# Weight sums of a seven-product layer in another order, and the down products' operands made in pieces between products

## The chip, the cores and the metric

One core of one Trainium2 chip runs one launch of the kernel. The metric is the device time of that launch in microseconds (us), the median over the runs shown. Engines are named as in the profile: PE (matrix unit), PEld (its weight loads), DVE (vector), ACT (scalar), POOL (GpSimd), SP (the queue that issues most DMAs).

## What is computed

The reference is one layer of a decoder for 1024 prompt tokens and 8 x 4 decode tokens, 1056 in all, model width 1024, everything in float32. Cut to the part in which the change lies:

```
mix = concat([attention(...), pooling(...)]) @ w_out
x = x + rms(mix, n_mix_post)
f = rms(x, n_ffn_pre)
f = (silu(f @ w_gate) * (f @ w_up)) @ w_down        # 1024 -> 2816 -> 1024
x = x + rms(f, n_ffn_post)
x = x + sigmoid(x @ w_ple_gate) * (p @ w_ple)
```

## The kernel before, in words

Tokens lie in three groups of 352 columns (g = 0, 1, 2). Features lie on the 128 partitions. Every float32 factor is split into a rounded part and a rest (`split`, line 172: a cast on ACT, then a difference on DVE), and a product term is three matmuls: part by part, part by rest, rest by part. One matmul is 128x128 by 128x352.

For groups 0 and 1 the products run two by two in a fast scheme with seven products in place of eight (`seven`, line 1085). The left matrix A has four blocks: the row is one 128-column chunk of `w_gate` (first raw tile, `a1`) or of `w_up` (second raw tile, `a2`), the column is one half of the 1024 inputs. The right matrix B has the input half as its row and the token group as its column. The seven products of such a **pair** are taken in this order: A11 B11, A12 B21, A22 T4, S2 T2, S3 T3, S1 T1, S4 B22, with S1 = A21+A22, S2 = S1-A11, S3 = A11-A21, S4 = A12-S2 (`T1` to `T4` are sums of the right side, made once). Each product is 12 matmuls (`product`), so a pair is 84. Group 2 uses plain products (`do_one`, `do_dn_one`).

The 22 chunks of the hidden width are worked in slabs of four (`SLAB`). In a slab s of the pair stage, the steps are pair 0, pair 1, down pair 0, pair 2, down pair 1, pair 3: 6 x 84 = 504 matmuls. A **down pair** (`do_dn_pair`, line 1199) multiplies the hidden values of slab s-1 by `w_down`, again with seven products, each in two halves of six matmuls, and adds each half to an accumulator in SBUF (`ap`; by DVE at line 1221, in the first slab by ACT at line 1223). Two pairs of a last, short slab and the last two down pairs end the stage. The names in the profile: `wr` is a raw weight tile, `wh`/`wl` the split of the whole first tile, `w` the split of A22 (the half product), `sh`/`sl` the split of the sums, `fh`/`fl` the right side, `hf` the hidden values of groups 0 and 1, `hp` the operands made of them for the down pairs, `b` a PSUM bank (8 of them).

**Weights.** SP loads raw tiles of 512 KB into three buffers in turn; the split tiles lie in eight buffers in turn. `need` makes the items four ahead of the one that is used: the sums of a pair are made during the pair before. `w_sums` (line 1044) runs four POOL operations in place (line 1054), two sums into each raw tile, then splits the two tiles (lines 1056 to 1059).

**Order.** PE's products are kept in program order. On the other engines a scheduler of the framework places the instructions when the kernel is built; each engine then runs its own list strictly in order. A wait of one instruction holds all behind it.

**Operands of the down pairs.** After pair 3 of a slab `h_operands` (line 1134) makes seven operands, B11, B21, B22 and the sums T1, T3, T2, T4: seven ACT casts, seven DVE differences (`hp`) and four DVE sums into `hf` (line 1131).

**Chains.** Work that should run between products can be written as a generator. `chain` registers it; `turn(n)`, called after every product, moves a counter on by n and lets a generator whose time has come issue its next piece; its next due time is its load divided by `share[0]`. `finish` issues at once what is left.

The functions that the change touches, and what calls them, are printed here with the line numbers of the profile:

Of the kernel before, what the change touches and what calls it, by code (L numbers as in the profile page):

```python
# [13 lines left out]
ALU = mybir.AluOpType  # L14
# [23 lines left out]
NSLAB = FFC // SLAB  # L38
# [24 lines left out]
def trunk_kernel(  # L63
# [33 lines left out]
    te, ve, se, ge = nc.tensor, nc.vector, nc.scalar, nc.gpsimd  # L97
# [14 lines left out]
    def act_tile(shape, dt=F32, s="a"):  # L112
        return apool.tile(shape, dt, tag="a", bufs=A_SLOTS, name=nm(s))

    def half(g, dt=F32, s="h"):
        return act_tile([P, 4, NS[g]], dt, s)
# [15 lines left out]
    def bank():  # L132
        return psum.tile([P, 512], F32, tag="b", name=nm("b"))
# [38 lines left out]
    def split(hi, lo, src):  # L172
        fix(se.copy(hi, src))  # L173
        fix(ve.tensor_tensor(lo, src, hi.bitcast(F32), op=ALU.subtract))  # L174
# [11 lines left out]
    def w_tile(shape, s):  # L186
        return wpool.tile(shape, F32R, tag="wp", bufs=2 * W_PAIRS, name=nm(s))
# [127 lines left out]
    def need(k, ahead=LOOK):  # L315

        for i in range(len(made), min(k + ahead + 1, len(ITEMS))):
            kind, js = ITEMS[i]
            if kind == "direct":
                w_split(js[0])  # L320
                made[i] = pairs[js[0]]
            elif kind == "half":
                w_load(js[0])
                hl = two_in_one([P, 4, P])
                split(*hl, raws[js[0]][:, 4:8, :])
                made[i] = hl
            elif kind == "small":
                w_load(js[0])
                hl = two_in_one([P, 2, 256])
                split(*hl, raws[js[0]])  # L330
                made[i] = hl
            else:
                made[i] = w_sums(*(raws[ITEMS[j][1][0]] for j in js))
            for kind, js in ITEMS[i + 1 : i + 3]:
                if kind != "sums":
                    w_load(js[0])
        return made[k]

    def gemm(ps, ops, start=True, stop=True):

        last = len(ops) - 1
        for i, (wh, wl, xh, xl) in enumerate(ops):
            mm(ps, wh, xh, start=start and i == 0, stop=False)
            mm(ps, wh, xl, start=False, stop=False)
            mm(ps, wl, xh, start=False, stop=stop and i == last)
# [589 lines left out]
    chains = []  # L935

    share = [0.6]

    def turn(n):

        now[0] += n
        for ch in [ch for ch in chains if ch[2]] or list(chains):
            while ch in chains and ch[1] <= now[0]:
                try:
                    load, wait = next(ch[0])
                except StopIteration:
                    chains.remove(ch)
                    break
                dve[0] = max(dve[0], now[0]) + load / share[0]
                ch[1] = dve[0] + wait  # L950

    def chain(steps, wait=0, alone=False):

        chains.append([steps, now[0] + wait, alone])

    def finish(ch_list):
        for ch in ch_list:
            for _ in ch[0]:
                pass
            chains.remove(ch)  # L960
# [83 lines left out]
    def w_sums(a1, a2):  # L1044


        a11, a12, a21, a22 = a1[:, 0:4, :], a1[:, 4:8, :], a2[:, 0:4, :], a2[:, 4:8, :]
        for out, a, b, op in (
            (a22, a21, a22, ALU.add),
            (a21, a11, a21, ALU.subtract),  # L1050
            (a11, a22, a11, ALU.subtract),
            (a12, a12, a11, ALU.subtract),
        ):
            ge.tensor_tensor(out, a, b, op=op)  # L1054
        two = []
        for src in (a1, a2):
            hl = w_tile([P, KC, P], "sh"), w_tile([P, KC, P], "sl")
            split(*hl, src)
            two.append(hl)
        (s24, s31) = two  # L1060
        return {"S2": quarter(s24, 0), "S4": quarter(s24, 1), "S3": quarter(s31, 0), "S1": quarter(s31, 1)}

    def ops4(w, x):

# [2 lines left out]
    def quarter(w, h):  # L1067
        return tuple(t[:, 4 * h : 4 * h + 4, :] for t in w)
# [16 lines left out]
    def seven(items, x7, done):  # L1085

        ig, iu, is_ = items[:3]
        wg = need(ig)
        p1 = tmp(N, "p1")
        se.copy(p1, product(quarter(wg, 0), x7["B11"]))  # L1090
        c11 = tmp(N, "c11")
        add(c11, p1, product(quarter(wg, 1), x7["B21"]))
        done("C11", c11)
        p4 = product(need(iu), x7["T4"])
        s = need(is_)
        add(p1, p1, product(s["S2"], x7["T2"]))
        u3 = tmp(N, "u3")
        add(u3, p1, product(s["S3"], x7["T3"]))
        c21 = tmp(N, "c21")
        add(c21, u3, p4)  # L1100
        done("C21", c21)
        p5 = product(s["S1"], x7["T1"])
        add(u3, u3, p5)
        add(p1, p1, p5)
        done("C22", u3)
        add(p1, p1, product(s["S4"], x7["B22"]))
        done("C12", p1)
# [7 lines left out]
    def hid_put(g, s, i, ht):  # L1115
        if (g, s) not in hid:
            if s < NSLAB:
                hid[g, s] = half(g, F32R, "hid"), half(g, F32R, "hid")
            else:
                t = half(g, F32R, "hid")  # L1120
                hid[g, s] = t[:, :REST, :], t[:, REST : 2 * REST, :]
        hi, lo = hid[g, s]
        split(hi[:, i, :], lo[:, i, :], ht)

    def h_operand(name, src):
        t = act_tile([P, 2, 2, N], F32R, "hp")
        split(t[:, 0], t[:, 1], src)
        h7[name] = t[:, 0], t[:, 1]

    def h_sum(name, out, a, b):  # L1130
        ve.tensor_tensor(out, a, b, op=ALU.subtract)
        h_operand(name, out)

    def h_operands():
        b11, b21, b12, b22 = (hidf[g][:, 2 * k : 2 * k + 2, :] for g in (0, 1) for k in range(2))
        h_operand("B11", b11)
        h_operand("B21", b21)
        h_operand("B22", b22)
        h_sum("T1", b11, b12, b11)
        h_sum("T3", b12, b22, b12)  # L1140
        h_sum("T2", b22, b22, b11)
        h_sum("T4", b21, b21, b22)

    def do_pair(s, i, items):

        t = {}

        def done(which, c):
            t[which] = c
            if which in ("C11", "C12"):  # L1150
                se.activation(c, c, AF.Silu)
            if which == "C11" and i == 0 and s < NSLAB:
                for g in (0, 1):
                    hidf[g] = half(g, s="hf")
            for g, a, b in ((0, "C21", "C11"), (1, "C22", "C12")):
                if which == ("C21", "C12")[g]:
                    if s < NSLAB:
                        ve.tensor_tensor(hidf[g][:, i, :], t[a], t[b], op=ALU.mult)
                    else:
                        ve.tensor_tensor(t[a], t[a], t[b], op=ALU.mult)  # L1160
                        hid_put(g, s, i, t[a])

        seven(items, f7, done)
        if s < NSLAB and i == SLAB - 1:
            h_operands()

    def do_one(s, i, items):
        if (s, i) == (AHEAD, 0):
# [28 lines left out]
    accp = {}  # L1197

    def do_dn_pair(s, j, items):
        ia, ib, is_ = items  # L1200
        for at, which, h, x in (
            (1, ia, 0, "B11"),
            (2, ia, 1, "B21"),
            (4, ib, None, "T4"),
            (6, is_, "S2", "T2"),
            (7, is_, "S3", "T3"),
            (5, is_, "S1", "T1"),
            (3, is_, "S4", "B22"),
        ):
            w = need(which)  # L1210
            w = w if h is None else w[h] if which == is_ else quarter(w, h)
            xh, xl = h7[x]
            if at not in accp:
                accp[at] = half(0, s="ap")
            for r in range(2):
                ps = bank()
                gemm(ps[:, :N], [(w[0][:, 2 * c + r, :], w[1][:, 2 * c + r, :], xh[:, c, :], xl[:, c, :]) for c in range(2)])
                turn(6)
                o = accp[at][:, 2 * j + r, :]
                if s:  # L1220
                    ve.tensor_tensor(o, o, ps[:, :N], op=ALU.add)  # L1221
                else:
                    se.copy(o, ps[:, :N])  # L1223
# [10 lines left out]

    def do_spill():
        finish(list(chains))

    def do_spill_sums():
        for d, t in zip(osd, os_[2]):
            nc.sync.dma_start(d, t)  # L1240
# [113 lines left out]
    def do_ple_one(m, wp, w):  # L1354
# [6 lines left out]
    do = {  # L1361
        "one": do_one,
        "pair": do_pair,
        "dn_one": do_dn_one,
        "dn_pair": do_dn_pair,
        "dn_rest": do_dn_rest,
        "combine": do_combine,
# [99 lines left out]
```

## Time and profile before

| what | value |
|---|---|
| three runs, median (lowest to highest) | 1133.71 us (1133.09 to 1134.46) |
| the profiled execution, its own time | 1133.11 us |
| its span, first to last instruction | 1131.3 us |
| busy: PE, PEld, DVE, ACT, POOL | 1097.9, 1074.9, 843.6, 505.5, 262.4 us |
| mean granted TensorE clock | 0.989 |

A busy PE is not a PE at its peak: a matmul is shown with 0.32 us, though the next one starts 0.16 us after it. So idle time shows only where a gap is long, and time lost is better read from how many matmuls a stretch holds. "Idle before, releaser" is the time in which an engine stood still before an instruction, and what ended it.

### The profile page before, as it was taken

The page shows a single profiled execution, that of the slowest core. Times are in us where ns is not written, and L with a number is a line of the kernel's source. Part 1 is how long each engine was busy: PE and PEld are TensorE (multiplying, and loading weights), DVE is VectorE, ACT ScalarE, POOL GpSimd, SP SyncE. Part 2 cuts the span into 40 slices and gives each one's busy share as a digit, 9 for nine tenths or more (in the row PEclk, how much of TensorE's full clock was granted, in tenths as well). Part 3 has the DMA queues.
Part 4 walks back from the last instruction along what each step waited for, and adds up shares of the span by engine and source line. Part 5 has one row for each costly group of instructions (what it writes and reads, how often), then busy time and mean ns, then how long its engine had stood idle before and what let it go on. Part 6 is the DMA issues. An engine that isn't in the chain of part 4 may idle for free. (4 is left out here: it accounts for less than half of the span.)

```text
span 1131.3 us, 17864 instructions
## 1 busy us (share of the span) xinstructions
PE 1097.9 (97%) x6979; PEld 1074.9 (95%) x6979; DVE 843.6 (75%) x1298; ACT 505.5 (45%) x863; POOL 262.4 (23%) x212
## 2 busy tenths in 40 slices
PE   9999999999999999989989989989988999999998
PEld 9999988899999999989989989989987999999998
DVE  6776578877969766765677777777788987968973
ACT  7322377655555433435433433333344364444441
POOL 0072132100000123243343343343332000012300
PEclk9999999999999999999999989999999999999999
DMA  8121311634633324222212212212234456553362
GB/s 285 59 71 52 106 57 39 204 132 145 233 131 131 112 97 142 75 75 76 75 66 84 76 40 92 76 54 75 76 100 164 153 182 214 190 202 105 132 190 75
DMA packets 43573, 131.29 MB, mean 116 GB/s; under 512 B 5060, under 2 KB 15588, under 8 KB 43488
## 3 DMA queue, kind: packets, MB, share of 16 engines
q1 hardware_dynamic: 42160, 128.38, 33.4%
q10 hardware_dynamic: 1328, 1.77, 0.5%
q8 instruction: 55, 0.90, 0.3%
q14 instruction: 30, 0.25, 0.1%
HBM read 114.25 MB, written 15.87 MB: 115 GB/s over the span
## 5 line engine op out<-in xcount | busy, mean ns | idle before, releaser
L1054 POOL TENSOR_TENSOR wr<-wr 128x512 f32<-128x512 f32 x72 | 101.9, 1415 | 650.3 <-DVE w L174 647.5
L173 ACT CAST wh<-wr 128x1024 fp32r<-128x1024 f32 (+1 forms) x138 | 142.0, 1030 | 153.7 <-PE b L128 75.1
L128 PE MATMUL b<-fh,wh 128*128 128x352 f32 x624 | 201.6, 323 | 1.4 <-ACT ap L1223 1.4
L128 PE MATMUL b<-fh,wl 128*128 128x352 f32 x624 | 200.2, 321 | 0.0
L128 PE MATMUL b<-fl,wh 128*128 128x352 f32 x624 | 200.0, 320 | 0.0
L174 DVE TENSOR_TENSOR wl<-wr,wh 128x1024 fp32r<-128x1024 f32 (+1 forms) x138 | 168.0, 1218 | 33.7 <-ACT wh L173 32.6
L174 DVE TENSOR_TENSOR sl<-wr,sh 128x1024 fp32r<-128x1024 f32 x72 | 87.4, 1222 | 125.5 <-ACT sh L173 121.7
L173 ACT CAST sh<-wr 128x1024 fp32r<-128x1024 f32 x72 | 72.9, 1048 | 193.7 <-POOL wr L1054 193.7
L128 PE MATMUL b<-fh,sh 128*128 128x352 f32 x416 | 138.8, 334 | 13.1 <-ACT sh L173 12.2
L128 PE MATMUL b<-fh,sl 128*128 128x352 f32 x416 | 138.1, 332 | 3.7 <-DVE sl L174 3.7
L128 PE MATMUL b<-fl,sh 128*128 128x352 f32 x416 | 137.1, 329 | 0.0
L128 PEld LDWEIGHTS b<-fh,wh 128*128 128x128 f32 x624 | 117.0, 188 | 1.7 <-ACT ap L1223 1.7
L128 PEld LDWEIGHTS b<-fl,wh 128*128 128x128 f32 x624 | 117.4, 188 | 0.0
L128 PEld LDWEIGHTS b<-fh,wl 128*128 128x128 f32 x624 | 117.0, 188 | 0.0
L128 PE MATMUL b<-h,wh 128*128 128x352 f32 x480 | 105.7, 327 | 0.3 <-ACT h L426 0.3
L1054 POOL TENSOR_TENSOR wr<-wr,wr 128x512 f32<-128x512 f32 x72 | 102.2, 1420 | 5.6
L128 PE MATMUL b<-hid,wh 128*128 128x352 f32 x416 | 99.5, 322 | 0.0
L128 PEld LDWEIGHTS b<-fh,sh 128*128 128x128 f32 x416 | 81.1, 195 | 15.1 <-ACT sh L173 14.0
L128 PEld LDWEIGHTS b<-fh,sl 128*128 128x128 f32 x416 | 81.1, 195 | 5.6 <-DVE sl L174 5.6
L128 PE MATMUL b<-hp,sh 128*128 128x352 f32 x320 | 78.9, 329 | 7.5 <-DVE ap L1221 4.2
L128 PEld LDWEIGHTS b<-h,wh 128*128 128x128 f32 x480 | 82.7, 191 | 1.1 <-ACT h L426 0.6
L128 PEld LDWEIGHTS b<-fl,sh 128*128 128x128 f32 x416 | 81.4, 196 | 0.0
(195 smaller groups left out, 2231.5 us busy)
## 6 DMA issues: line engine op xcount, KB each, us to landing
wr<-in_w_gu_dram SPq DMA_DIRECT2D x88, 512.0 KB, 3.4
wr<-in_w_dn_dram SPq DMA_DIRECT2D x40, 512.0 KB, 3.3
wr<-in_w_pg_dram SPq DMA_DIRECT2D x16, 512.0 KB, 3.6
x<-in_x_dram SPq DMA_DIRECT2D x6, 704.0 KB, 9.3
x1d<-x SPq DMA_DIRECT2D x6, 704.0 KB, 3.5
x<-x1d SPq DMA_DIRECT2D x6, 704.0 KB, 5.5
out_y_dram<-yo SPq DMA_DIRECT2D x24, 176.0 KB, 2.9
wr<-in_w_out_b_dram SPq DMA_DIRECT2D x8, 512.0 KB, 3.8
```

The lines of the kernel that those rows point to most:

```text
L128: ins = te.matmul(*args, **kw)
L173: fix(se.copy(hi, src))
L174: fix(ve.tensor_tensor(lo, src, hi.bitcast(F32), op=ALU.subtract))
L1054: ge.tensor_tensor(out, a, b, op=op)
```

## The change

In `w_sums` the four sums are written in another way and order: S3 = A11-A21 and then S2 = A22-S3, both into the second raw tile, which is split at once; then S1 = A11+S2 and S4 = A12-S2 into the first raw tile, split second. S2 and S3, which PE takes first, lie in one split tile, S1 and S4 in the other. The order of PE's products is the same. `h_operands` becomes a generator of seven pieces, registered as a chain after pair 3 and finished at the latest at C21 (the fifth product) of the next slab's pair 0, where now also the new `hf` tiles are taken, or ahead of down pair 0. From the spill on, `share[0]` is 0.9.

```diff
         a11, a12, a21, a22 = a1[:, 0:4, :], a1[:, 4:8, :], a2[:, 0:4, :], a2[:, 4:8, :]
-        for out, a, b, op in (
-            (a22, a21, a22, ALU.add),
-            (a21, a11, a21, ALU.subtract),
-            (a11, a22, a11, ALU.subtract),
-            (a12, a12, a11, ALU.subtract),
+        two = []
+        for src, steps in (
+            (a2, ((a21, a11, a21, ALU.subtract), (a22, a22, a21, ALU.subtract))),
+            (a1, ((a11, a11, a22, ALU.add), (a12, a12, a22, ALU.subtract))),
         ):
-            ge.tensor_tensor(out, a, b, op=op)
-        two = []
-        for src in (a1, a2):
+            for out, a, b, op in steps:
+                ge.tensor_tensor(out, a, b, op=op)
             hl = w_tile([P, KC, P], "sh"), w_tile([P, KC, P], "sl")
             split(*hl, src)
             two.append(hl)
-        (s24, s31) = two
-        return {"S2": quarter(s24, 0), "S4": quarter(s24, 1), "S3": quarter(s31, 0), "S1": quarter(s31, 1)}
+        s32, s14 = two
+        return {"S2": quarter(s32, 1), "S4": quarter(s14, 1), "S3": quarter(s32, 0), "S1": quarter(s14, 0)}
...
     def h_operands():
         b11, b21, b12, b22 = (hidf[g][:, 2 * k : 2 * k + 2, :] for g in (0, 1) for k in range(2))
-        h_operand("B11", b11)
-        h_operand("B21", b21)
-        h_operand("B22", b22)
-        h_sum("T1", b11, b12, b11)
-        h_sum("T3", b12, b22, b12)
-        h_sum("T2", b22, b22, b11)
-        h_sum("T4", b21, b21, b22)
+        for name, b in (("B11", b11), ("B21", b21), ("B22", b22)):
+            h_operand(name, b)
+            yield 6, 0
+        for name, *args in (
+            ("T1", b11, b12, b11),
+            ("T3", b12, b22, b12),
+            ("T2", b22, b22, b11),
+            ("T4", b21, b21, b22),
+        ):
+            h_sum(name, *args)
+            yield 11, 0
...
-            if which == "C11" and i == 0 and s < NSLAB:
-                for g in (0, 1):
+            if which == "C21" and i == 0:
+                finish(list(chains))
+                for g in (0, 1) if s < NSLAB else ():
                     hidf[g] = half(g, s="hf")
...
         if s < NSLAB and i == SLAB - 1:
-            h_operands()
+            chain(h_operands(), 6)
...
     def do_dn_pair(s, j, items):
+        if j == 0:
+            finish(list(chains))
...
     def do_spill():
         finish(list(chains))
+        share[0] = 0.9
```

**On POOL**, these are the sums of two pairs, pair 0 and pair 1 of slab 4 (`wr_7100` and `wr_7235` hold `w_gate`, `wr_7146` and `wr_7280` hold `w_up`). Before:

```order
L1054 TENSOR_TENSOR wr_7146<-wr_7146 128x512
L1054 TENSOR_TENSOR wr_7146<-wr_7100,wr_7146 128x512
L1054 TENSOR_TENSOR wr_7100<-wr_7146,wr_7100 128x512
L1054 TENSOR_TENSOR wr_7100<-wr_7100 128x512
L1054 TENSOR_TENSOR wr_7280<-wr_7280 128x512
L1054 TENSOR_TENSOR wr_7280<-wr_7235,wr_7280 128x512
L1054 TENSOR_TENSOR wr_7235<-wr_7280,wr_7235 128x512
L1054 TENSOR_TENSOR wr_7235<-wr_7235 128x512
```

The same two groups in the changed kernel:

```order
L1054 TENSOR_TENSOR wr_7146<-wr_7100,wr_7146 128x512
L1054 TENSOR_TENSOR wr_7146<-wr_7146 128x512
L1054 TENSOR_TENSOR wr_7100<-wr_7100,wr_7146 128x512 x2
L1054 TENSOR_TENSOR wr_7280<-wr_7235,wr_7280 128x512
L1054 TENSOR_TENSOR wr_7280<-wr_7280 128x512
L1054 TENSOR_TENSOR wr_7235<-wr_7235,wr_7280 128x512 x2
```

There are four operations to a group as before. The first no longer touches A22, which the split `w` reads; the second does, and completes the tile that is split first. The last two read the second raw tile, which before only the first three did.

**On DVE**, this is the stretch in which the operands of slab 3 are made, about pair 0 of slab 4 (`wl_7296` is the split of pair 1's first tile, `w_7387` that of its A22). Before:

```order
L1131 TENSOR_TENSOR hf_6607<-hf_6607 128x704
L174 TENSOR_TENSOR wl_7296<-wr_7235,wh_7295 128x1024
L174 TENSOR_TENSOR hp_7368<-hf_6607,hp_7368 128x704
L174 TENSOR_TENSOR hp_7372<-hf_6606,hp_7372 128x704
L174 TENSOR_TENSOR hp_7376<-hf_6607,hp_7376 128x704
L1131 TENSOR_TENSOR hf_6607<-hf_6607,hf_6606 128x704
L174 TENSOR_TENSOR w_7387<-wr_7280,w_7387 128x512
L1131 TENSOR_TENSOR hf_6606<-hf_6606,hf_6607 128x704
L174 TENSOR_TENSOR hp_7380<-hf_6607,hp_7380 128x704
L1083 TENSOR_TENSOR c_7407<-p_7392,b_7408 128x352
L174 TENSOR_TENSOR hp_7384<-hf_6606,hp_7384 128x704
L1083 TENSOR_TENSOR p_7392<-p_7392,b_7456 128x352
```

The same place in the changed kernel (`w_7362` is the A22 split, `sl_7407` the rest of the tile with S3 and S2):

```order
L1129 TENSOR_TENSOR hf_6669<-hf_6669 128x704
L174 TENSOR_TENSOR wl_7296<-wr_7235,wh_7295 128x1024
L1081 TENSOR_TENSOR c_7385<-p_7367,b_7386 128x352
L174 TENSOR_TENSOR w_7362<-wr_7280,w_7362 128x512
L174 TENSOR_TENSOR hp_7431<-hf_6669,hp_7431 128x704
L174 TENSOR_TENSOR hp_7452<-hf_6668,hp_7452 128x704
L1081 TENSOR_TENSOR p_7367<-p_7367,b_7438 128x352
L174 TENSOR_TENSOR hp_7474<-hf_6669,hp_7474 128x704
L1129 TENSOR_TENSOR hf_6669<-hf_6669,hf_6668 128x704
L174 TENSOR_TENSOR sl_7407<-wr_7280,sh_7406 128x1024
L1081 TENSOR_TENSOR u_7456<-p_7367,b_7457 128x352
L1129 TENSOR_TENSOR hf_6668<-hf_6668,hf_6669 128x704
```

The split `w`, which POOL waits for, stood behind three `hp` and one sum; now it stands behind one eviction (`c`), and the `hp` and sums come after it, among the evictions. Seven `hp` and four sums are made in both.

## The prediction

> **What bounds the kernel now.** The page comes first: PE is busy nearly all the time. So the stretches were read by their matmul counts, in the answer by windows, cut where the waits end; beside it one row of the chain of waits, a run of PE without a break.
>
> ```profile
> PE 1097.9 (97%) x6979; PEld 1074.9 (95%) x6979; DVE 843.6 (75%) x1298; ACT 505.5 (45%) x863; POOL 262.4 (23%) x212
> ...
> 871.30 148.28 PE b L128 x933
> ...
> 484.00:574.63 90.63, 84.04 (x517) 82.63 (x516) 52.73 (x72) 42.41 (x73) 35.33 (x26) 1.00 0.22 70
> 574.63:662.33 87.70, 83.58 (x505) 82.11 (x505) 64.67 (x100) 31.55 (x44) 33.96 (x24) 0.98 0.22 73
> 662.33:749.95 87.62, 83.70 (x504) 82.64 (x504) 64.95 (x100) 31.55 (x44) 33.86 (x24) 0.96 0.22 73
> 749.95:837.58 87.63, 83.29 (x505) 81.78 (x505) 64.96 (x100) 31.57 (x44) 33.86 (x24) 0.98 0.22 73
> 837.58:873.00 35.42, 29.94 (x160) 28.29 (x161) 30.40 (x46) 15.50 (x21) 12.13 (x8) 0.90 0.47 161
> 873.00:1030.00 157.00, 157.00 (x992) 157.00 (x991) 136.49 (x193) 75.98 (x101) 5.16 (x4) 1.00 0.53 184
> 1030.00:1082.00 52.00, 49.37 (x297) 48.17 (x296) 44.36 (x66) 22.22 (x32) 17.19 (x12) 0.97 0.36 117
> ```
>
> Columns: window, length, then PE, PEld, DVE, ACT, POOL busy (instructions), granted clock, DMA. The unbroken run gives 148.28 / 933 = 0.159 us per matmul. A slab of 504 needs 80.1 us and takes 87.6. The five windows from 484 to 873 hold 2191 matmuls, 348.2 us of work, and last 389.0: **40.8 us are lost there**. From 873 to 1030 nothing is lost (992 x 0.159 = 157.7). From 1030 to 1082, 297 matmuls need 47.2 of 52.0 us: 4.8 lost. After 1082 the sums are over. PE bounds the kernel except in these two stretches, so 45.6 us is all that this change can win: floor 1133.1 - 45.6 = 1087.5.
>
> What PE waits for there, PE's waits from 484 to 873:
>
> ```profile
> PE b L128 <- ACT sh L173: 12.2, 5, 3.3
> PE b L128 <- DVE ap L1221: 4.5, 4, 3.4
> PE b L128 <- DVE sl L174: 3.0, 5, 0.7
> PE b L128 <- ACT ap L1223: 2.9, 2, 1.5
> PE b L128 <- DVE p L1083: 1.7, 4, 0.9
> ```
>
> Twenty waits, 24.3 us. The `sh` and `sl` waits are ten in five places, once per slab. Behind them stands a slowed clock:
>
> ```profile
> 501.58:504.99 3.41, 2.13 (x13) 2.16 (x14) 2.85 (x6) 1.94 (x4) 0.00 (x0) 1.00 0.57 167
> ...
> 576.67:580.09 3.42, 3.42 (x13) 3.42 (x12) 3.28 (x7) 0.96 (x3) 0.00 (x0) 0.50 0.79 255
> 662.00:665.42 3.42, 2.79 (x8) 2.33 (x9) 3.08 (x4) 2.52 (x4) 0.00 (x0) 0.50 0.26 74
> 665.42:668.83 3.41, 3.41 (x14) 3.41 (x13) 3.31 (x7) 1.02 (x2) 0.00 (x0) 0.50 0.73 238
> 750.75:754.17 3.42, 2.96 (x10) 2.96 (x11) 3.36 (x6) 1.40 (x3) 0.00 (x0) 0.50 0.52 166
> 839.50:842.91 3.41, 3.41 (x14) 3.41 (x13) 3.38 (x7) 1.37 (x3) 0.00 (x0) 0.50 0.85 235
> 859.98:863.39 3.41, 2.79 (x10) 2.82 (x11) 3.10 (x6) 1.37 (x1) 2.98 (x3) 0.50 0.89 370
> 1040.88:1044.30 3.42, 3.42 (x13) 3.42 (x12) 2.78 (x7) 2.55 (x4) 0.00 (x0) 0.50 0.47 153
> ...
> 836.09:839.50 3.41, 1.25 (x6) 0.96 (x7) 1.94 (x2) 3.02 (x4) 0.36 (x1) 1.00 0.00 0
> ```
>
> Each window at 0.50 loses its busy time less 0.159 per matmul: 1.35, 1.52, 1.19, 1.37, 1.18, 1.20, together 7.8 us before 873, and 1.35 at 1040.88. Each follows a long wait: the window before 839.50 has 1.25 us of PE work in 3.41; the one at 501.58, with a wait but 2.13 us of work, is followed by full clock.
>
> So the 40.8 us are 24.3 of waits, 7.8 of clock, and about 20 x 0.27 = 5.4 beside the waits (after one, PE also lacks the overlap, 0.32 against 0.16, and its second start comes 0.27 later, not 0.16); 3.3 stay unassigned.
>
> **Why the weights come late.** The wait that ends at 749.95, in order of time, with its releasers (PE, DVE, POOL, ACT):
>
> ```profile
> 749.95 0.43 PE L128 MATMUL b<-fh,sh 128*128 128x352 f32 x1 [3.30 <-ACT sh L173]
> ...
> 737.57 2.49 DVE L174 TENSOR_TENSOR hp<-hf,hp 128x704 fp32r<-128x704 f32 x3
> 739.98 0.88 DVE L1131 TENSOR_TENSOR hf<-hf,hf 128x704 f32<-128x704 f32 x1
> 740.78 0.68 DVE L174 TENSOR_TENSOR w<-wr,w 128x512 fp32r<-128x512 f32 x1
> ...
> 742.98 0.51 DVE L1083 TENSOR_TENSOR c<-p,b 128x352 f32<-128x352 f32 x1
> 743.42 1.55 DVE L174 TENSOR_TENSOR hp<-hf,hp 128x704 fp32r<-128x704 f32 x1
> ...
> 741.59 2.62 POOL L1054 TENSOR_TENSOR wr<-wr 128x512 f32<-128x512 f32 x1 [12.01 <-DVE w L174]
> 744.30 3.18 POOL L1054 TENSOR_TENSOR wr<-wr,wr 128x512 f32<-128x512 f32 x2
> 747.56 1.26 POOL L1054 TENSOR_TENSOR wr<-wr 128x512 f32<-128x512 f32 x1
> ...
> 748.86 1.99 ACT L173 CAST sh<-wr 128x1024 fp32r<-128x1024 f32 x2 [4.83 <-POOL wr L1054]
> ...
> 730.70 1.23 DVE L174 TENSOR_TENSOR sl<-wr,sh 128x1024 fp32r<-128x1024 f32 x1 [3.63 <-ACT sh L173]
> ```
>
> A22's split `w` stands behind three `hp` and a sum, the four POOL sums wait for `w`, the cast `sh` waits for all four, and PE, free since 749.95 - 3.30 = 746.65, for the cast. The last row shows DVE standing 3.63 us before another `sl`: its queue is held, with the evictions behind it, until POOL is done. That makes the `ap` waits.
>
> **The change, part by part.**
>
> *Sums.* No instruction comes or goes: four POOL sums, two casts, two differences, the same DMAs. From the end of `w` to the cast, four sums stood (741.59 to 748.82, 7.2 us; 5.5 at the usual speed). In the order of the changed kernel S3 needs no `w` and can run ahead; one sum remains, 1.26 to 2.62 us. The first tile is ready 4.2 to 6 us sooner. The second keeps its place within a sum, and PE needs it two products (24 x 0.159 = 3.8 us) later than the first. SP's load of the next second tile waited for the first tile's `sl`, behind four sums; now for that `sl` and for the last sum, which reads this tile too; the sums end no later than before, and cast and difference (1.05, 1.23) no longer stand behind them: earlier by about 2 us, and SP queues nothing new.
>
> *Pieces.* `w` now stands behind one `c` (0.51) in place of 2.49 + 0.88: 2.9 us sooner. The seven casts, seven `hp` and four sums remain, among the evictions. They cost PE nothing while its eight banks last, and that cover shows in the trace. The first product of pair 0 starts here, and its bank is copied here:
>
> ```profile
> 727.42 0.32 PE L128 MATMUL b<-fh,wh 128*128 128x352 f32 x1
> ...
> 734.79 0.44 ACT L1090 COPY p<-b 128x352 f32<-128x352 f32 x1
> ```
>
> Twelve matmuls end at 729.3, the copy comes 5.5 us later, and PE did not wait. What is left at C21 (two sums, two or three `hp`, 4.4 us) holds the evictions behind it by no more than that. If the cover fails, the same 4.4 us stand in each of five slabs, 22 us; if the pieces fill holes, nothing. I take 0.
>
> *Both together at 749.95.* `w` ends about 738.6, the sum at latest 741.2, `sh` 742.3, `sl`, behind three `hp` and a sum, 745. PE needs it at 746.65. **All five places go**: 12.2 + 3.0 + 10 x 0.27 = 17.9 us; I keep 0.4 of it. With no long wait left, the **clock's 7.8 us go** too.
>
> *Down pairs.* 4.5 + 2.9 + 1.7 + 10 x 0.27 = 11.8 us. They end when DVE or ACT, held by `sh` and POOL, evict late. The second `sl` still stands in those queues, so I take two thirds, 7.8 (bounds 0 and 11.8). Of the unassigned 3.3 I take none (bounds 0 and 3.3).
>
> *From 1030.* The pairs of the last stage use the same sums:
>
> ```profile
> PE b L128 <- DVE acc L850: 1.1, 1, 1.1
> PE b L128 <- DVE p L1332: 0.9, 1, 0.9
> PE b L128 <- DVE sl L174: 0.7, 1, 0.7
> ...
> 1037.21 1.23 DVE L174 TENSOR_TENSOR sl<-wr,sh 128x1024 fp32r<-128x1024 f32 x1 [2.27 <-ACT sh L173]
> ```
>
> That `acc` runs right behind this `sl`. It and the `sl` wait go with the 1.35 of clock: 1.1 + 0.7 + 0.5 + 1.35 = 3.7 (bounds 0 and 4.8).
>
> Sum: 17.5 + 7.8 + 7.8 + 3.7 = 36.8 from the profiled execution's 1133.1: 1096.3. Its time is 0.6 under the median 1133.7; I split that and say 1096.5.
>
> *A rule against the change.* At 741.59 a sum took 2.62 us, and at 743.42 an `hp` 1.55 where three others took 2.49 together: they block each other. The Trainium skill ("SBUF — State Buffer", SBUF: two separate sides) says that GpSimd and a DVE operation with two SBUF inputs share a port pair under an exclusive lock, held for a whole instruction. These rows agree. Outside the page's words: by the rows a sum costs DVE at most 0.7 us, by a lock held for every sum 1.41; both prices stand in the third rival. In the forecast I take nothing for it, since DVE has 80.1 - 64.95 = 15 us to spare in a slab (bounds 0 and that rival's 7 us).
>
> **Rivals.**
>
> *The second split takes over the block.* DVE and ACT are then held by the second `sh` as long as before, and only the pair waits and their clock go. For it: the queues are strict and the second tile comes hardly earlier. Against: the 3.63 us holes are at the first `sl`. Kept then: 11.8 - 4.0 of the down pairs' loss, the clock at 859.98 (1.2) and the 3.7: 1096.5 + 7.8 + 1.2 + 3.7 = 1109.
>
> *The clock windows stay.* Were they not made by these waits, 7.8 + 1.35 would stay: 1105.5. Against: the pattern above. The Trainium skill ("TensorE: Matmul & The Clock Gate", Part 1) has the clock halve after an idle window of about 3.4 us and restore after a busy one; by that none of the windows before, which all hold some work, would start it. The row at 836.09 shows a part idle window enough.
>
> *DVE becomes the bound; the slower side.* Sums and DVE differences now run side by side instead of in turn. A slab has 24 sums and 64.95 us of DVE work. An `hp` lost 1.55 - 0.83 = 0.7 us to one sum: 24 x 0.7 = 17, 81.8 us per slab against PE's 80.1; over 4.4 slabs (389 / 87.6) about 7 us, 1104. Slower than before it gets once each sum costs DVE over (87.63 - 64.95) / 24 = 0.95 us; at a whole sum each time (33.86 / 24 = 1.41) a slab lasts 98.8, 11.2 more than now: 1133 + 4.4 x 11.2 = 1182. Against: evictions read PSUM and in the rows above (`c` at 742.98, 0.51) lose nothing.
>
> *The change does nothing*, because loads and not sums make the weights late: 1133. Against: the releasers are POOL and ACT, not a DMA.
>
> **How the numbers follow.** Chances: forecast 0.68; second split 0.13; DVE at the bound, 1104, 0.07; clock stays 0.05; DVE slower 0.05; nothing 0.02. The low end is the floor, 1087; the high end 1111 takes in the second split, the clock, DVE at the bound and no gain in the down pairs. Outside stay slower and nothing, and a tail. Over 0.2% (2.3 us, about what a measurement here can tell): faster 0.93, same 0.02, slower 0.05.
>
> **What the changed profile would show.** Right: slabs near 80 us in 504 matmuls; no wait of PE for `sh`; no window at 0.50 between 484 and 873; DVE idle before `sl` much below 3.6 us; POOL sums longer than now. Wrong: slabs over 84 us; PE waiting for `ap` or `p`; DVE busy all through a slab; half clock without a wait before it.

## The result and the profile after

| | before | after |
|---|---|---|
| median, us | 1133.4 (4 runs) | 1093.79 (4 runs, 1093.51 to 1095.91) |
| profiled execution, us | 1133.1 | 1093.8 |
| ratio | | 0.9654, 95% interval 0.9638 to 0.9671 |

39.6 us went; the time is 2.7 below the forecast 1096.5. The page of the changed kernel, engine line:

```profile
PE 1080.0 (99%) x6979; PEld 1063.7 (97%) x6979; DVE 874.5 (80%) x1298; ACT 511.4 (47%) x863; POOL 284.4 (26%) x212
```

DVE is 30.9 us busier than before and POOL 22.0, for the same instructions; PE 17.9 less, in part because fewer windows run at half clock. The chain of waits shows more: two runs of PE hold 826 of 1092 us, and the first of them covers the pair stage up to 783 us (start, length, count).

```profile
218.65 564.72 PE b L128 x3567
...
826.67 261.24 PE b L128 x1632
```

564.72 / 3567 is 0.158 us per matmul. The windows by slab, cut where a slab begins (same columns as before; the row at 813.14 is the last down pairs, the last one stands for 1030 to 1082 of before):

```profile
492.20:572.90 80.70, 80.70 (x510) 80.70 (x509) 57.57 (x72) 43.06 (x73) 38.86 (x25) 1.00 0.24 79
...
733.06:813.14 80.08, 80.08 (x506) 80.02 (x505) 72.14 (x101) 33.68 (x46) 38.22 (x25) 1.00 0.26 89
813.14:835.00 21.86, 17.12 (x93) 16.55 (x92) 18.62 (x28) 9.83 (x13) 9.30 (x6) 0.84 0.43 160
...
992.00:1044.00 52.00, 52.00 (x330) 52.00 (x329) 51.34 (x82) 27.95 (x41) 17.75 (x11) 1.00 0.46 152
```

A slab lasts 80.08 instead of 87.6, PE never pauses in it, the clock is full. DVE has 72.1 us of work in it, 7.2 more than before, and still 8 us to spare. PE's longest waits in the whole execution:

```profile
PE b L128 <- DVE ap L1226: 4.0, 1, 4.0
PE b L408 <- POOL c L156: 1.6, 1, 1.6
PE b L128 <- DVE p L1081: 0.7, 1, 0.7
```

The rest are 0.7 us and less, and none is for `sh` or `sl`. One place is left, 813 to 835, where the last down pairs begin. The right side of group 2 is loaded again there (`fr`) and split (`fh`, `fl`) for the plain products that come behind these pairs; these are the reloaded operands of the text below. The timeline there, DVE then PE:

```profile
819.74 1.22 DVE L174 TENSOR_TENSOR sl<-wr,sh 128x1024 fp32r<-128x1024 f32 x1
820.87 0.52 DVE L1081 TENSOR_TENSOR p<-p,b 128x352 f32<-128x352 f32 x1
821.30 2.27 DVE L174 TENSOR_TENSOR fl<-fr,fh 128x1408 fp32r<-128x1408 f32 x1
...
823.93 1.21 DVE L174 TENSOR_TENSOR wl<-wr,wh 128x1024 fp32r<-128x1024 f32 x1
...
825.50 0.68 DVE L174 TENSOR_TENSOR w<-wr,w 128x512 fp32r<-128x512 f32 x1
826.11 2.66 DVE L1226 TENSOR_TENSOR ap<-ap,b 128x352 f32<-128x352 f32 x6
...
821.44 0.58 PE L128 MATMUL b<-hp,sh 128*128 128x352 f32 x2 [0.74 <-DVE p L1081]
826.67 0.66 PE L128 MATMUL b<-hp,sh 128*128 128x352 f32 x1 [4.00 <-DVE ap L1226]
```

Six evictions (`ap`) stand behind the difference of a reloaded operand (`fl`, 2.27 us), a product of hidden values (`u`) and three splits. By the gaps between matmul starts PE pauses 0.9 and 4.3 us, and the clock stands at 0.50 from 824.35 to 831.17, which costs 2.0 us more: with 0.1 beside them 7.3 us in one place.

### The profile page after: what moved, and what is told of

Read it like the earlier page. It is cut to its first block, busy times and chain, and to the rows that moved or that the text cites. A ratio compares the mean times of both kernels' runs of the same rounds, so it can differ in the third digit from the quotient of the medians.

```text
span 1092.0 us, 17927 instructions
## 1 busy us (share of the span) xinstructions
PE 1080.0 (99%) x6979; PEld 1063.7 (97%) x6979; DVE 874.5 (80%) x1298; ACT 511.4 (47%) x863; POOL 284.4 (26%) x212
## 4 chain that ended last, share of the span: by engine, by line
PE 91%; DVE 4%; DMA 2%; issue 1%; ACT 1%; POOL 1%; SPq 0%; DVEq 0%; POOLq 0%; ACTq 0%
PE b L128 90%; PE b L122 1%; DMA xr<-in_x_dram 1%; DMA a<-in_dmask_dram 1%; POOL wr L1054 1%; DVE sl L174 0%; SPq L402 0%; DVE wl L174 0%; DVE mx L693 0%; ACT xr L436 0%; DVE a L801 0%; ACT wh L173 0%; DVE hf L1129 0%; DVE h L428 0%; ACT h L426 0%
## 5 line engine op out<-in xcount | busy, mean ns | idle before, releaser
L1054 POOL TENSOR_TENSOR wr<-wr,wr 128x512 f32<-128x512 f32 x108 | 175.0, 1636 | 484.3 <-DMA wr<-in_w_gu_dram 217.3
L173 ACT CAST sh<-wr 128x1024 fp32r<-128x1024 f32 x72 | 75.7, 1051 | 139.2 <-POOL wr L1054 131.5
L128 PE MATMUL b<-fh,sh 128*128 128x352 f32 x416 | 134.3, 323 | 0.0
L128 PE MATMUL b<-fl,sh 128*128 128x352 f32 x416 | 133.2, 320 | 0.0
L128 PE MATMUL b<-fh,sl 128*128 128x352 f32 x416 | 133.2, 320 | 0.0
L174 DVE TENSOR_TENSOR sl<-wr,sh 128x1024 fp32r<-128x1024 f32 x72 | 96.1, 1336 | 36.8 <-ACT sh L173 18.5
L1054 POOL TENSOR_TENSOR wr<-wr 128x512 f32<-128x512 f32 x36 | 51.0, 1418 | 106.5 <-DVE w L174 106.5
L128 PEld LDWEIGHTS b<-fl,sh 128*128 128x128 f32 x416 | 78.2, 188 | 0.0
L128 PEld LDWEIGHTS b<-fh,sh 128*128 128x128 f32 x416 | 78.0, 188 | 0.0
L128 PEld LDWEIGHTS b<-fh,sl 128*128 128x128 f32 x416 | 77.9, 187 | 0.0
```

What stands on the lines that cost most here:

```text
L128: ins = te.matmul(*args, **kw)
```

## The experiments

Experiments 1 to 4, 5 to 8 and 9 to 12 form three groups. The kernels of a group ran on one chip beside runs of the kernel before (median 1132.8 to 1133.5 in the three groups), and each ratio is to these.

### 1. The new order of sums alone

The kernel before with the new `w_sums`; `h_operands` stays one block after pair 3. As an edit of the changed kernel, cut (the places of `finish`, of the `hf` tiles and of `share[0]` go back too):

```
-        for name, b in (("B11", b11), ("B21", b21), ("B22", b22)):
-            h_operand(name, b)
-            yield 6, 0
+        h_operand("B11", b11)
...
-            chain(h_operands(), 6)
+            h_operands()
```

> Only the new order of the weight sums; the seven operands of the down products are made in one block at C21, as before. Theory A (the first tile came too late by one path, the operand block ahead of A22's split and then four sums, and any 2.5 us off that path closes the gap): two or three sums, 4.2 us or more, leave it, PE's five waits for sh and sl end, the half-clock windows behind them too, and the waits for ap and p in the down pairs shrink by less than half: 1133.4 - 17.9 - about 6.5 of clock - 0 to 5 = 1104 to 1109; PE waits for sh under 1 us in sum. Rival B (each part brings its own share, and the operand block is the larger one, since it also holds the evictions): under 12 us of gain, 1121 or more, PE still waits 5 us or more for sh.

Measured: 1093.59 us, ratio 0.9649 (0.9633 to 0.9664). **The new order alone is the whole gain.** The timeline where the operand block stands in a slab, DVE, POOL, ACT, PE:

```profile
715.51 0.68 DVE L174 TENSOR_TENSOR w<-wr,w 128x512 fp32r<-128x512 f32 x1
...
720.07 1.34 DVE L174 TENSOR_TENSOR sl<-wr,sh 128x1024 fp32r<-128x1024 f32 x1 [1.83 <-ACT sh L173]
...
716.34 2.61 POOL L1054 TENSOR_TENSOR wr<-wr 128x512 f32<-128x512 f32 x1 [6.40 <-DVE w L174]
719.03 3.53 POOL L1054 TENSOR_TENSOR wr<-wr,wr 128x512 f32<-128x512 f32 x2
...
718.99 1.05 ACT L173 CAST sh<-wr 128x1024 fp32r<-128x1024 f32 x1 [2.58 <-POOL wr L1054]
...
725.65 0.32 PE L128 MATMUL b<-fh,sh 128*128 128x352 f32 x1
```

The split `w` still stands behind most of the block, but one sum (716.34) follows it and then the cast. `sh` ends at 720.04, 5.6 us ahead of its product. DVE stands 1.83 us before `sl`, where it stood 3.6 to 3.9 in the kernel before. Theory A put this kernel 10 to 15 us too high: it took at most 5 us for the down pairs and nothing for the stretch from 1030 or for the unassigned 3.3, and these went too.

### 2. The operands in pieces alone

An edit of the changed kernel, its first lines; the four sums, the splits and what `w_sums` returns go back to those of the kernel before:

```
-        for src, steps in (
-            (a2, ((a21, a11, a21, ALU.subtract), (a22, a22, a21, ALU.subtract))),
-            (a1, ((a11, a11, a22, ALU.add), (a12, a12, a22, ALU.subtract))),
+        for out, a, b, op in (
+            (a22, a21, a22, ALU.add),
...
```

> Only the operands in pieces (and the two ends of chains and the share that go with it); the four weight sums stand in the old order, all ahead of the first cast. Theory A: A22's split comes 2.9 us sooner, the waits for sh were 2.4 us on average, so these waits fall below 0.5 us each, and the down pairs, which no block holds, lose their ap waits: 1098 to 1108. The two parts alone then gain more together than both at once (39.6 us). Rival B: the four sums still hold cast and difference, PE still waits for sh 1 us or more in each slab, the first sl holds DVE 3 us or more and with it the evictions: 1113 to 1124.

Measured: 1127.82 us, ratio 0.9952 (0.9935 to 0.9968). Rival B's picture, with even less gain than it gave. Down pair 0 of a slab in the timeline, DVE and POOL, and PE's waits for `p` from 750 to 764:

```profile
750.77 0.68 DVE L174 TENSOR_TENSOR w<-wr,w 128x512 fp32r<-128x512 f32 x1
...
758.36 1.23 DVE L174 TENSOR_TENSOR sl<-wr,sh 128x1024 fp32r<-128x1024 f32 x1 [3.63 <-ACT sh L173]
759.50 0.51 DVE L1083 TENSOR_TENSOR u<-u,b 128x352 f32<-128x352 f32 x1
759.93 0.52 DVE L1083 TENSOR_TENSOR p<-p,b 128x352 f32<-128x352 f32 x1
...
751.69 1.29 POOL L1054 TENSOR_TENSOR wr<-wr 128x512 f32<-128x512 f32 x1 [9.77 <-DVE w L174]
753.06 2.82 POOL L1054 TENSOR_TENSOR wr<-wr,wr 128x512 f32<-128x512 f32 x2
755.96 1.29 POOL L1054 TENSOR_TENSOR wr<-wr 128x512 f32<-128x512 f32 x1
```

```profile
PE b L128 <- DVE p L1083: 2.9, 2, 2.6
```

Four sums in a row still stand between `w` and the cast, DVE stands 3.63 us, and two evictions wait behind `sl`; PE waits 2.6 us for the second of them. Over the execution PE's waits for `sh` did fall, from 12.2 us to 3.2, much as theory A had it, but those for `p` rose from 1.7 to 9.2, and those for `ap` stayed, 7.0 after 7.4. The wait moved from the product to the bank. So the pieces bring 5 us alone and, from experiment 1 against the changed kernel (1093.59 against 1093.79), nothing that these runs can tell beside the new order.

### 3. Matmuls in the wait: the clock

An edit of the kernel before:

```
+        if fill_now[0]:
+            ps = bank()
+            for _ in range(fill_now[0]):
+                mm(ps[:, :N], x7["B11"][0][:, 0, :P], x7["B11"][0][:, 0, :], start=True, stop=True)
...
+        fill_now[0] = 14 if s >= 2 and i == 1 else 0
         seven(items, f7, done)
+        fill_now[0] = 0
```

> The kernel before, with 14 additional matmuls (2.2 us of work, into a bank that nothing reads) ahead of the product that waits for sh, in pair 1 of the slabs from the third on: they fill part of the wait and bring nothing to the result. Theory C (the half clock comes because PE is idle for most of a window): at three or four of the five places PE is active in 2.5 us or more of each 3.41 us window, the windows at 0.50 behind them vanish, 1.2 to 1.4 us each; the matmuls themselves fit into the waits (2 to 3.3 us): 1127 to 1131. Rival D (the clock steps down whatever fills the wait, by a limit on load or heat): the windows stay, and the time is 1133 to 1137.

Measured: 1136.06 us, ratio 1.0028 (1.0018 to 1.0039). The time went to rival D's side, the windows to theory C's: at all four places with the additional matmuls the clock stayed full, and it fell behind other waits. Windows of one 3.41 us step each, a place that was filled and one that was not:

```profile
573.43:576.84 3.41, 2.20 (x12) 1.62 (x11) 1.99 (x2) 3.07 (x4) 0.31 (x1) 1.00 0.00 0
576.84:580.25 3.41, 3.41 (x23) 3.37 (x22) 3.27 (x7) 1.05 (x3) 0.00 (x0) 1.00 0.76 244
...
675.79:679.20 3.41, 1.30 (x9) 1.01 (x7) 2.20 (x4) 2.94 (x3) 0.09 (x1) 1.00 0.00 0
679.20:682.61 3.41, 3.38 (x12) 3.41 (x13) 3.41 (x7) 1.12 (x2) 0.00 (x0) 0.50 0.88 290
```

At the filled place PE is busy 2.20 us and the clock stays; at the other 1.30 us, and it halves. The time rose because 56 matmuls (8.9 us) filled waits that in part moved on: one wait of 4.7 us for `c` in the down pair behind 853 is new, and its window, without a single matmul, brought half clock too. By the gaps between matmul starts from 484 to 873 (875 here), the two kernels' balances are 31.0 of pauses and 8.2 of clock before, 29.1, 5.1 and 8.9 of filling here: 3.9 more, against 3.3 measured. That too little matmul work in a window brings the half clock is shown (the last section has the limit); that filling pays is not, here.

### 4. The reloaded operands, three times

First in the changed kernel, as steps of a chain; then (8) the same edit on the new order of sums alone; then (12) on that with four half pieces. Cut:

```
-    def do_reload():
+    def reload_steps():
         for h in range(2):
             t = half(2, s="fr")
             nc.sync.dma_start(t, fsd[h])
+            yield 0, 40
+            fixed[0] = True
             fs[2][h] = f_operand(t, 2)
+            fixed[0] = False
+            yield 0, 10
+
+    def do_reload():
+        chain(reload_steps(), 30)
```

> The changed kernel, with the two operands that the last down pairs reload made in steps, so that the first evictions of that stage (ap) stand ahead of both of their differences on DVE, one of them even behind sl. After loses 7.3 us there: waits of 0.9 and 4.3 us at 821.4 and 826.7 and 2.0 us of half clock behind them. Theory E (the reloaded operand's difference, 2.27 us, and the splits behind it hold the evictions): the 4.3 us wait falls under 1 us and the half clock goes, 1087.5 to 1090. Rival F (the evictions wait for the products or the bank anyway, or the reloaded operand itself is then late for its product): the wait only moves to fh or fl, 1092 to 1096.

Measured: 1090.19 us, ratio 0.9624 (0.9605 to 0.9643). The 4.0 us wait fell to two, 3.1 us in all, and no half clock stands there: theory E's cause, and a little less than its gain (it had under 1 us of wait and 1087.5 to 1090). The two whole differences still stand before evictions, one ahead of `w` and one behind `sl`.

> The new order of sums and the reloaded operands in steps, and the down products' operands in one block as in the kernel before. The program now places both differences of the reloaded operands behind ten and seventeen evictions, the first one behind both sl. If the pieces are worth nothing beside the new order: no later than the changed kernel with the reload in steps (1090.2), and since fewer long operations stand ahead of the evictions the last 3.1 us of ap waits go as well: 1087 to 1089. If the pieces gave cover somewhere that the one run does not show: 1091 or more, with new waits for p or ap at a block of hp.

Measured: 1092.16 us, ratio 0.9638 (0.9622 to 0.9655). No new wait for `p` or `ap` came, so the expectation "1091 or more" fits in time and not in cause. Now the operand itself was late for the first product that reads it, at 846.95, and the only half clock of the stage came there:

```profile
PE b L128 <- DVE fl L174: 3.3, 1, 3.3
```

The twelfth kernel loads both operands first and splits them by halves:

```
+    def reload_steps():
+        fr = [half(2, s="fr") for _ in range(2)]
+        for h in range(2):
+            nc.sync.dma_start(fr[h], fsd[h])
+        for h in range(2):
+            hi, lo = fs[2][h] = half(2, F32R, "fh"), half(2, F32R, "fl")
+            for k in (0, 2):
+                yield 0, 10
+                fixed[0] = True
+                split(hi[:, k : k + 2, :], lo[:, k : k + 2, :], fr[h][:, k : k + 2, :])
+                fixed[0] = False
...
+        chain(reload_steps(), 6)
```

> The new order of sums alone, the operands of the down products in one block, and the reloaded operands in four half pieces whose differences (0.8 us each) stand between the evictions: the first behind A22's split, the others behind the second sl. Before this, both whole in front left 4.0 us of ap wait and 2.0 to 2.7 of half clock, in steps beside the pieces 3.1 of ap wait, and far behind 3.3 of fl wait and 2.6 of half clock. Theory E: with neither the evictions nor the reloaded operand late, under 1 us of PE waits between 484 and 873: 1086 to 1088.5, the floor of the slabs. Rival: one of the two is late again, 1089 to 1092.

Measured: **1088.25 us, ratio 0.9601 (0.9588 to 0.9614)**, the fastest of all, 5.5 us under the changed kernel and without its pieces. Its waits for evictions (theory E had under 1 us), a slab, and the last down pairs:

```profile
PE b L128 <- DVE ap L1219: 1.1, 2, 0.7
```

```profile
564.00:644.00 80.00, 80.00 (x505) 80.00 (x505) 68.75 (x100) 32.39 (x44) 37.72 (x24) 1.00 0.23 79
...
804.00:860.00 56.00, 54.85 (x342) 54.30 (x341) 54.54 (x78) 22.63 (x31) 13.49 (x8) 1.00 0.44 157
```

That is theory E's range, and near the prediction's floor of 1087.5. It also shows that what was left in the changed kernel was this one place.

### 5 and 6. Two and four sums ahead of the cast

An edit of experiment 1's kernel:

```
-            (a2, ((a21, a11, a21, ALU.subtract), (a22, a22, a21, ALU.subtract))),
-            (a1, ((a11, a11, a22, ALU.add), (a12, a12, a22, ALU.subtract))),
+            (a2, ((a21, a11, a21, ALU.subtract), (a22, a22, a21, ALU.subtract), (a11, a11, a22, ALU.add))),
+            (a1, ((a12, a12, a22, ALU.subtract),)),
```

In the sixth all four stand in the first line.

> The kernel with the new order of sums alone, but S1 is summed ahead of the first cast: two sums stand between A22's split and the cast (new order 1, old order 4), the order of the sums, their number and POOL's instructions unchanged. Theory G (the number of sums between A22's split and the first cast is what counts: it sets how long DVE stands before sl with the evictions behind it, 1.2 to 1.8 us in the new order, 3.6 in the old; the first tile came 5.6 us before its product in the new order): DVE stands 2.5 to 3.3 us, PE waits for no sh, evictions begin to be late by 0 to 1 us in some places, 1094 to 1104. Rival H (it is enough that S3 runs ahead of the split): 1093.6, DVE stands no longer than 1.8.

> The same with all four sums ahead of the first cast: three between A22's split and the cast. Theory G: DVE stands 3.5 us or more as in the kernel before, most of the waits come back, as evictions (ap, p, c) rather than sh, because the first tile still comes 1.4 us sooner than in the old order: 1108 to 1130. Rival H: 1095 or less. Rival B2 (only PE's waits for sh count, and the 5.6 us of slack cover two more sums of 1.3 to 1.8 us): 1094 to 1097.

Measured: 1093.0 (0.9631 to 0.9664) and 1092.88 us (0.9630 to 0.9662), as experiment 1. They didn't test what they were made for. ACT and POOL in the sixth:

```profile
731.47 1.05 ACT L173 CAST sh<-wr 128x1024 fp32r<-128x1024 f32 x1 [1.75 <-POOL wr L1054]
...
729.93 1.50 POOL L1054 TENSOR_TENSOR wr<-wr 128x512 f32<-128x512 f32 x1 [2.26 <-DVE w L174]
731.51 3.53 POOL L1054 TENSOR_TENSOR wr<-wr,wr 128x512 f32<-128x512 f32 x2
```

The cast runs right behind S2 (it ends at 731.43), with two sums still to come: it waits for the sums that write its tile, wherever the code puts it, and POOL's order was already S3, S2, then the other two. So it isn't where the cast is written that makes the first tile early. Its two sums come first in POOL's queue, and one of them needs no `w`.

### 7. More sums on POOL: the price for DVE

An edit of the changed kernel:

```
+    junk = const([P, TB, P])
...
+        for _ in range(2):
+            ge.tensor_tensor(junk, diag, diag, op=ALU.add)
```

> The changed kernel with two additional POOL sums of 128x384 on a tile of their own ahead of each group of four, 12 to a slab; nothing reads them. Lock theory (a POOL sum of 128x512 costs DVE about 0.3 us, by 72.1 against 64.95 us of DVE work in a slab for 24 sums): DVE grows by 12 x 0.75 x 0.3 = 2.7 us to about 75 per slab, still under PE's 80.1, and the slabs stay at 80.1: 1093 to 1096. Rival (a lock of the whole sum, 1.0 us each): DVE grows by about 12 us to 84, slabs longer than 83, 1105 or more.

Measured: 1117.01 us, ratio 0.9859 (0.9840 to 0.9878). The time is the rival's and the place is neither's: the added sums depend on nothing, so the program put all 72 at the start, and the slabs, which they didn't touch, still last 80.1 us. The group, and the first 87 us:

```profile
L1051 POOL TENSOR_TENSOR c<-c 128x384 f32<-128x384 f32 x72 | 76.7, 1065 | 5.3
```

```profile
0.00:87.00 87.00, 70.63 (x367) 66.73 (x368) 70.91 (x78) 33.02 (x55) 81.11 (x100) 0.90 0.37 123
```

The changed kernel does 106 DVE instructions in these 87 us in 62.7 busy us, this one 78 in 70.9. Over the execution DVE is 29.8 us busier (904.3 against 874.5) for 76.7 us of added sums. PE did 367 matmuls there instead of 512; it waits 10.5 us in four waits for DVE (`dg`), in the changed kernel 0.5. The run gives the price of one of these sums, 1.07 us long, beside dense DVE work, 0.4 us, and says nothing on the slabs.

### 9 to 11. More sums between the split and the first cast

The ninth is an edit of experiment 1's kernel:

```
-            (a2, ((a21, a11, a21, ALU.subtract), (a22, a22, a21, ALU.subtract))),
+            (a2, ((a21, a11, a21, ALU.subtract), (a22, a22, a21, ALU.subtract), (a22, a22, a12, ALU.add), (a22, a22, a12, ALU.subtract))),
```

In the tenth the two additional steps stand twice; the eleventh has two of them and the operands in pieces.

(The "two kernels before" of the first text are 5 and 6.)

> The new order of sums alone, with two additional POOL sums behind S2 that add A12 and take it off again: three sums now stand between A22's split and the first cast, where the new order has one and the old had four (the two kernels before this one did not change that: their first cast still ran right behind S2). Theory G (this number decides): the first tile comes 2.8 to 3.5 us later, still 1.5 to 2.5 us ahead of its product, but DVE stands 4 us or more ahead of sl, as long as in the kernel before, and evictions come late: PE waits for p, c, u or ap of 1 to 3 us in most pairs, 1105 to 1128. Rival H (it is enough that S3 runs ahead of the split, or that POOL's other sums stand behind the first cast): 1097 or less.

> The same with four additional sums, five between A22's split and the first cast, one more than in the old order; the sums are 8 to a pair, so POOL works about 74 us of a slab. Theory G: the first tile comes 5.6 to 7 us later than in the new order and so 0.5 to 1.5 us after its product, DVE stands 6 to 7 us, PE waits for sh again in every slab: 1135 to 1165, slower than the kernel before. Rival H: 1105 or less.

> The changed kernel (operands in pieces too) with the two additional sums. If the pieces are a reserve that shows only where the sums leave no slack, this is 3 to 12 us faster than the same sums with the operands in one block. If they have no effect at all, both are the same within 2 us; slower is possible, since the pieces let DVE stand with more evictions behind it.

Measured: 1170.17 (ratio 1.0321, 1.0307 to 1.0336), 1267.20 (1.1182, 1.1167 to 1.1197) and 1167.75 us (1.0301, 1.0286 to 1.0317). Theory G's direction, and its price more than twice as high as its top; rival H is out. The ninth at the operand block, DVE, ACT and PE:

```profile
672.40 0.68 DVE L174 TENSOR_TENSOR w<-wr,w 128x512 fp32r<-128x512 f32 x1
...
680.16 1.32 DVE L174 TENSOR_TENSOR sl<-wr,sh 128x1024 fp32r<-128x1024 f32 x1 [3.60 <-ACT sh L173]
681.40 0.51 DVE L1081 TENSOR_TENSOR p<-p,b 128x352 f32<-128x352 f32 x1
...
679.09 1.04 ACT L173 CAST sh<-wr 128x1024 fp32r<-128x1024 f32 x1 [4.38 <-POOL wr L1054]
...
682.06 0.63 PE L128 MATMUL b<-fh,sh 128*128 128x352 f32 x1 [4.63 <-DVE p L1081]
```

PE stops at 677.4 (682.06 - 4.63). `sh` ends at 680.13, 2.7 us late and not 1.5 to 2.5 early as theory G had it. The two sums are not why: from the end of `w` to the end of the cast it takes 7.1 us here and 3.9 in experiment 1, 3.2 more, as theory G put it. But `w` itself, in a queue that had just stood 4.24 us for the `sl` at 659.37, now ends only 4.4 us ahead of the time at which PE stops, where in experiment 1 it ended 9.5 us ahead of its product. And PE starts only when the eviction `p` is done at 681.9, and that stands behind `sl`, which stood 3.60 us for POOL. In the kernel before, with four sums, DVE stood 3.89 us at this place of a later slab, but `p` was ahead of `sl`, and PE waited 3.2 us, for `sh`:

```profile
832.53 0.51 DVE L1083 TENSOR_TENSOR p<-p,b 128x352 f32<-128x352 f32 x1
833.14 0.52 DVE L1083 TENSOR_TENSOR u<-p,b 128x352 f32<-128x352 f32 x1
837.56 2.36 DVE L174 TENSOR_TENSOR sl<-wr,sh 128x1024 fp32r<-128x1024 f32 x2 [3.89 <-ACT sh L173]
```

So at this place three sums cost more than four did, by what stands behind the waiting difference. Over the whole execution it is the same: the ninth kernel's PE waits 52.6 us for evictions (`p` 26.4, `ap` 14.3, `u` 7.6, `c` 4.3) and never for `sh` or `sl`; in the kernel before it was 10.0 for evictions and 15.9 for `sh` and `sl`. From 484 to 912 the ninth kernel loses 59 us in pauses and 15 in clock. DVE's waits for the cast before `sl` in the whole execution order most of the kernels, but not all (us): changed 18.5, sums alone 24.8, pieces alone 105.5, before 121.7, two more 138.0, four more 229.1; and pieces with two more 116.9 at 1167.75. Whether the order of DVE's queue accounts for all that this measure leaves was not tried, and why three sums cost so much more than four did before stays open to that extent. The pieces take 2.4 us off the ninth, and the two intervals overlap: little or nothing, even where the sums leave no slack.

## Why the prediction was right, point by point

- **The bound and the floor: right.** PE bounds, the two stretches held what could be won, and experiment 12 came to 1088.25 against a floor of 1087.5.
- **Sums, four ahead of the cast becoming one: right, and it was everything.** The five `sh` and `sl` places went with it alone. From the end of `w` to the end of the cast it took 8.45 us at 749.95 and takes 3.85 in experiment 1: 4.6 less, and the prediction said 4.2 to 6.
- **Pieces, "2.9 us sooner": about true, and worth nothing.** Without the pieces `sh` is there 5.6 us ahead of its product (experiment 1), with them 8.6 (in the changed kernel the cast ends at 717.56, its product starts at 726.12); `w` itself comes 2.1 us sooner (11.6 us ahead against 9.5). The prediction put both shifts into one sum and took the pieces as needed ("both together at 749.95"); either shift alone was longer than the 2.4 us that an average place waited, but they are not alike: the shorter chain also frees DVE's queue, the earlier `w` doesn't (experiment 2). That step failed, without harm to the number. Its cost, 0, was right in time; in DVE's work the pieces add 3.2 us a slab (72.1 against 68.9).
- **Down pairs, 7.8 of 11.8: mis-sized, and the reason failed.** "The second `sl` still stands in those queues" wasn't the limit. The standing at the first `sl` held the evictions, and with it gone nothing was left in any slab: 6.5 of the 11.8 came. What was left stands at the last down pairs, the 3.4 us `ap` wait of the profile before, whose cause, the reloaded operands, the prediction did not see: 5.3 of pauses and 2.0 of clock.
- **Clock, 7.8: right as a mechanism,** shown by experiment 3; 5.8 came, 2.0 stayed at that place.
- **Unassigned, 0 of 3.3: all 3.3 came back**, the slabs have nothing left. **From 1030, 3.7: 5.4**, more than the upper bound of 4.8. That bound took 0.159 us for every matmul, and six of those near 1039 are one column wide. **Kept 0.4: nothing.**
- The balance: both kernels run the same 6979 matmuls, so their start times can be set side by side. The changed kernel is level with the kernel before at the matmul that starts there at 484, 34.0 us ahead at 873, 34.0 at 1030, 39.3 at 1082, and no further ahead at the end. So the two stretches hold the whole 39.3 us by which the two profiled executions differ. The terms give 45.6 - 7.3 = 38.3, about 0.5 too little in each stretch.
- **Part of the closeness is luck.** The clock and the down pairs were taken 3.3 us too high; the unassigned part and the stretch from 1030 were taken 5.0 too low.
- **DVE, the rule against the change: the price is there, and DVE has room for it.** By the single `hp` a sum was to cost at most 0.7; measured (72.1 - 64.95) / 24 = 0.30 with pieces and (68.9 - 64.95) / 24 = 0.16 without. For DVE to bound the slabs it had to be (80.1 - 64.95) / 24 = 0.63, for a slower kernel the third rival's 0.95.
- **The signs.** The slabs last 80.08, PE waits for no `sh`, DVE stands at most 2.6 us for the cast before `sl`, and a POOL sum of two tiles takes 1636 ns instead of 1420: all as forecast. "No window at 0.50 between 484 and 873" failed, at 824.35 and 827.76, and one sign of being wrong showed at the same place: PE waits 4.0 us for `ap`.

## What to carry to other kernels

When an engine with a strict queue waits for a chain on another engine, count the steps of that chain and what stands behind the waiting instruction; the step that shortens the chain pays twice, at the consumer and at the evictions held behind it. Bringing the chain's start forward without shortening it only moved the wait from the operand to the bank. Before crediting two parts of a change, compare each with the slack that the other one leaves.

## What the runs showed of the hardware

The changed kernel's own half clock, window by window, and a window of the kernel before that was also followed by half clock:

```profile
820.93:824.35 3.42, 1.23 (x6) 0.94 (x6) 3.42 (x5) 1.32 (x3) 1.17 (x1) 1.00 0.68 231
824.35:827.76 3.41, 1.09 (x4) 1.09 (x5) 3.41 (x7) 0.28 (x2) 1.33 (x2) 0.50 1.00 410
827.76:831.17 3.41, 3.41 (x13) 3.41 (x12) 2.17 (x4) 2.74 (x3) 2.47 (x2) 0.50 0.35 147
831.17:834.58 3.41, 3.41 (x23) 3.41 (x23) 3.40 (x6) 0.53 (x1) 0.00 (x0) 1.00 0.19 43
...
1037.47:1040.88 3.41, 2.33 (x17) 2.04 (x16) 3.41 (x4) 2.34 (x4) 0.00 (x0) 1.00 0.28 77
```

- The clock halves after a 3.41 us window in which PE did too little, and is back after a full one. The busy column does not show the limit well. 1.23 us (here, 820.93), 1.25 (before, 836.09), 1.30 (experiment 3) and 1.75 (experiment 7, 843.53) brought the clock down, and so did 2.33 (before, 1037.47; the prediction's row at 1040.88 is the next window). 1.59 (experiment 2, 756.42) and 1.69 (before, 832.67) did not. The column counts a lone matmul as 0.32 us, and six of those in the window at 1037.47 are one column wide and shown as 0.83 us.
- Counted as 0.159 us for each matmul of 352 columns, and less by its columns for a narrow one, the fourteen traces agree. From 380 us on, all 54 windows at full clock with 1.31 us of such work or less were followed by half clock, and none of the 2876 with 1.43 or more. Three lie between, at 1.33, 1.33 and 1.37 (the one at 1037.47), and two of them were. So the limit is, as an estimate, 1.3 to 1.4 us of matmul work in 3.41, about two fifths. The Trainium skill ("TensorE: Matmul & The Clock Gate", Part 1) speaks of an idle window; here a window about a third busy was enough.
- A POOL sum's price for DVE depends on what runs beside it: `hp` took 979 ns on average before, 1042 with the new order, 1229 with pieces spread over the sums. Where DVE stands waiting for the sums, it costs next to nothing: 72 added sums in experiment 9 raised DVE's busy time from 863.6 to 865.4 us.
